# A one-operation reciprocal root in the context LayerNorm, and three more context FFN steps emitted ahead of the reload

## The chip, the cores and the metric

The kernel runs on one core of a Trainium2 chip. The metric is the device time of one execution in microseconds (us), lower is better. All times below come from one profiled execution of the kernel before, or from its three timed runs.

## The reference, cut to what matters

The program is one inference step of a two-layer backbone with two groups of tokens that share all weights: 128 context tokens (`xc`) and 1024 latent tokens (`xl`), of width 1024. Layer 0 mixes tokens with a state-space scan (S5), layer 1 with window pooling. Each layer ends in a SwiGLU FFN of width 2816, and each of the two sub-layers ends in a LayerNorm of the scaled residual.

```python
def layer_norm(x, g, b):
    mu = jnp.mean(xf, axis=-1, keepdims=True)
    var = jnp.mean(jnp.square(xf - mu), axis=-1, keepdims=True)
    y = (xf - mu) * lax.rsqrt(var + LN_EPS)
    return (y * g + b).astype(x.dtype)

def swiglu(h, w_gate, w_up, w_down):
    return (jax.nn.silu(h @ w_gate) * (h @ w_up)) @ w_down

# layer 0, for the context (c) and for the latent tokens (l):
oc, fin_re, fin_im = s5_mixer(hc, *params, zeros, zeros)      # scan, output tables, gelu, GLU
ol, _, _ = s5_mixer(hl, *params, state_re[:, j], state_im[:, j])
xc = layer_norm(DEEPNORM_ALPHA * xc + g1c * oc, ln_g[i, 0], ln_b[i, 0])
xl = layer_norm(DEEPNORM_ALPHA * xl + g1l * ol, ln_g[i, 0], ln_b[i, 0])
fc = swiglu(modulate(xc, sh2c, sc2c), ffn_w_gate[i], ffn_w_up[i], ffn_w_down[i])
fl = swiglu(modulate(xl, sh2l, sc2l), ffn_w_gate[i], ffn_w_up[i], ffn_w_down[i])
```

## The kernel before, in words

Activations lie with the channels on the 128 partitions and the tokens along the free dimension. The context is one block of 128 tokens (`C`), the latent tokens are two blocks of 512 (`A`, `B`). Context matmuls are plain fp32; the profile lists each as two records. Latent matmuls are split into three products of high and low parts (L844 to L846).

In layer 0 the order of the program around the change is this.

- **Scan.** `ssm_scan_lat` runs 127 dependent steps in two directions on VectorE (L477, L482). Beside it, `ctx0a` brings the context through its own GLU and its first LayerNorm (`ln_stats`, `ln_apply`). While `self.scanning` holds, the context's elementwise work goes to GpSimd (`elem`), and what GpSimd needs from PSUM is copied by ScalarE (`in_sb`). The LayerNorm ends in the modulated context `xmc` (L1014), on which every matmul of the context FFN waits. In it the reciprocal of the root is taken by GpSimd as a power of minus one (L993), after a Sqrt on ScalarE (L989); two multiplications by GpSimd then refine it by a Newton step, before (`lr`) and after this change alike.
- **Readout and reload.** `ssm_y` runs eight times (the tiles 6, 7, 5, 0, 1, 2, 3, 4). Each time it loads tables (`mo` of 1 MB into two buffers; `mk` of 0.5 MB), copies scan states into `sd` (L629, L631, L633), multiplies (`py`, L677 and L680), applies gelu on ScalarE (`yl`, L683) and stores to a scratch tensor `yd` (L686). After the last one the main program reloads `yd` in another layout as `yr` (L1200) and splits it (`xm`, `xn`); this is the reload.
- **GLU of the latent blocks.** `glu(A)` and `glu(B)` make eight output tiles each, and after each tile one step is taken from the iterator `fill`.

The context FFN of layer 0 is that iterator, `ctx0b`: 22 steps of `ffn_up` (16 matmuls and two weight loads of 512 KB each), 8 steps of `ffn_down` (22 matmuls each), and the second context LayerNorm at the 31st call. 15 steps are emitted ahead of the reload by `self.step(fill, 15)`; the 16 calls in the two GLUs take the rest. Steps ahead of the reload load their weights into the three buffers of the pool `raw`, those behind it into the small buffers `rc` (256 KB).

The program order is not the order on the engines: a scheduler of the framework with a simulated timeline places each engine's instructions, and every engine then runs its own list strictly in that order. The SyncE queue (SP) issues the loads, also in order. The first six `ffn_up` steps multiply on GpSimd, later ones on VectorE (L918, `hc`).

Of the kernel before, what the change touches and what calls it, by code (L numbers as in the profile page):

```python
# [11 lines left out]
F32 = mybir.dt.float32  # L12
F32R = mybir.dt.float32r
I32 = mybir.dt.int32
AF = mybir.ActivationFunctionType
OP = mybir.AluOpType
# [25 lines left out]
class Kernel:  # L42
# [920 lines left out]
    def ln_stats(self, b):  # L963

        nc = self.nc
        v = self.elem(b)
        n = b.n
        x = b.x
        t = b.tmp.tile([128, 2, n], F32, tag="lt" + b.tg, name="lt", bufs=3)
        v.tensor_tensor(t, x[:, 0:2], x[:, 2:4], op=OP.add)  # L970
        v.tensor_tensor(t, t, x[:, 4:6], op=OP.add)
        v.tensor_tensor(t, t, x[:, 6:8], op=OP.add)
        v.tensor_tensor(t[:, 0], t[:, 0], t[:, 1], op=OP.add)
        pm = self.in_sb(b, v, self.ones_mm(b, t[:, 0], "lnm"))
        acc = None
        for q in range(4):
            xq = x[:, 2 * q:2 * q + 2]
            v.tensor_tensor(xq, xq, pm.unsqueeze(1).to_broadcast([128, 2, n]), op=OP.subtract)
            sq = b.tmp.tile([128, 2, n], F32, tag="lt" + b.tg, name="sq", bufs=3)
            nc.scalar.activation(sq, xq, AF.Square)  # L980
            if acc is None:
                acc = sq
            else:
                v.tensor_tensor(acc, acc, sq, op=OP.add)
        v.tensor_tensor(acc[:, 0], acc[:, 0], acc[:, 1], op=OP.add)
        pv = self.ones_mm(b, acc[:, 0], "lnv")
        r = b.tmp.tile([128, n], F32, tag="lr" + b.tg, name="lr", bufs=1)
        q = b.tmp.tile([128, n], F32, tag="lq" + b.tg, name="lq", bufs=1)
        nc.scalar.activation(q, pv, AF.Sqrt, bias=self.eps if b.split else self.epsc[:, 0:1])  # L989
        if v is nc.vector:  # L990
            v.reciprocal(r, q)
        else:
            v.tensor_tensor(r, q, self.minus.to_broadcast([128, n]), op=OP.pow)  # L993
        self.stt(b, q, pv, LN_EPS / (ALPHA * ALPHA), r, OP.add, OP.mult, self.epsc[:, 0:1])
        self.stt(b, q, q, -0.5, r, OP.mult, OP.mult)
        self.stt(b, r, q, 1.5, r, OP.add, OP.mult)
        for q in range(4):
            xq = x[:, 2 * q:2 * q + 2]
            v.tensor_tensor(xq, xq, r.unsqueeze(1).to_broadcast([128, 2, n]), op=OP.mult)
# [158 lines left out]
    def build(self):  # L1158
        tc, nc = self.tc, self.nc
        with ExitStack() as st:  # L1160
# [15 lines left out]
            self.XC = P("xcres").tile([128, 8, 128], F32, name="XC")  # L1176
            self.gate, self.lnm = {}, {}
            self.scanning = False
            self.minus = self.cp.tile([128, 1], F32, name="minus")
            nc.vector.memset(self.minus, -1.0)  # L1180
            self.ident = self.cp.tile([128, 128], F32, name="ident")
            make_identity(nc, self.ident)
            self.ssm()
            fill = self.ctx0b()
            self.step(fill, 15)
            self.scanning = False
            self.whl = P("whl")
            xr = P("xres")
# [5 lines left out]
            with tc.tile_pool(name="xm1", bufs=1) as xmp:  # L1194
# [20 lines left out]
                with tc.tile_pool(name="adl", bufs=1, side="right") as adl:  # L1215
                    fill = self.ada_late(adl)
# [19 lines left out]
            fill = self.ctx1b()  # L1236
# [91 lines left out]
```

## Time and profile before

| | |
|---|---|
| timed runs | 2452.82, 2456.66, 2459.58 us (median 2456.66) |
| the profiled execution's own time | 2459.29 us |
| its span in the profile | 2457.3 us, 33344 instructions |
| TensorE (PE) busy | 2254.7 us, 92% of the span |
| VectorE (DVE), ScalarE (ACT), GpSimd (POOL) busy | 1281.1, 937.5, 284.2 us |
| mean granted TensorE clock | 0.958 of full speed |

The profiled execution took 2.6 us more than the median of the three runs. A stretch is read as follows: the busy time of each engine in it, the granted clock of TensorE as a share of its full 2.4 GHz, the share of the 16 DMA engines that was busy, and the rate at which they moved data. An instruction is read by its start, its duration, and in square brackets the idle time of its engine just before it and what ended that.

### The profile page before, as it was taken

To read this page: it belongs to the slowest core of one execution; us is meant where nothing else is said; L and a number is where in the kernel's file an instruction comes from. 1 tells how busy PE (TensorE), PEld (TensorE's weight loads), DVE (VectorE), ACT (ScalarE), POOL (GpSimd) and SP (SyncE) were. 2 spreads that over 40 slices of the span, in tenths; PEclk is the share of its full clock that TensorE was granted. 3 is DMA by queue.
4 is the path that set the end of the run, shared out by engine and by line. 5 is a ranking of instruction groups with operands and counts; after the bars stand their busy time and mean duration, and the time that the engine had idled before them with its cause. 6 is when DMAs were issued, how large, how long until landed. Compare 5 with 4: busy or idle time off the path is not lost.

```text
span 2457.3 us, 33344 instructions
## 1 busy us (share of the span) xinstructions
PE 2254.7 (92%) x13105; PEld 1871.8 (76%) x13105; DVE 1281.1 (52%) x2421; ACT 937.5 (38%) x1387; POOL 284.2 (12%) x338
## 2 busy tenths in 40 slices
PE   4896658799999999999999999889999999999996
PEld 2565648688887777788888888777788888888996
DVE  6779962344546222456223765677322456322476
ACT  2774234543225222544222544126222443322464
POOL 4921474300010000100000010001000100000000
PEclk7896879899999999999999999999999999999998
DMA  7877448864554554423333326773333232333452
GB/s 219 243 235 218 138 106 255 246 175 138 162 161 154 158 193 156 168 96 93 102 96 95 103 95 180 213 201 110 104 94 95 97 100 86 98 94 95 143 198 103
DMA packets 458012, 357.22 MB, mean 145 GB/s; under 512 B 14960, under 2 KB 405888, under 8 KB 455808
## 3 DMA queue, kind: packets, MB, share of 16 engines
q1 hardware_dynamic: 451920, 340.91, 46.2%
q0 software_dynamic: 3200, 8.39, 1.1%
q10 hardware_dynamic: 2736, 5.80, 0.6%
q8 instruction: 103, 1.69, 0.3%
q14 instruction: 53, 0.43, 0.1%
HBM read 336.58 MB, written 18.35 MB: 144 GB/s over the span
## 4 chain that ended last, share of the span: by engine, by line
PE 80%; DMA 11%; DVE 3%; ACT 2%; POOL 2%; issue 1%; SPq 0%; ACTq 0%; POOLq 0%; DVEq 0%
PE ffn L844 13%; PE ffn L846 13%; PE ffn L845 13%; PE dn L844 6%; PE dn L845 6%; PE dn L846 6%; PE ffn L848 4%; PE dn L848 3%; PE glu L845 2%; PE glu L846 2%; PE glu L844 2%; DMA adaw<-ada_w 2%; DMA raw<-ffn_w_gate 2%; DMA raw<-ffn_w_down 1%; DMA mo<-mo 1%
## 5 line engine op out<-in xcount | busy, mean ns | idle before, releaser
L828 ACT ACTIVATE wh<-raw 128x1024 fp32r<-128x1024 f32 (+1 forms) x326 | 341.5, 1049 | 947.7 <-PE ffn L845 623.4
L829 DVE TENSOR_TENSOR wl<-raw,wh 128x1024 fp32r<-128x1024 f32 (+1 forms) x326 | 394.3, 1210 | 500.1 <-ACT wh L828 491.8
L845 PE MATMUL dn<-hkl,wh 128*128 128x512 f32 (+1 forms) x880 | 304.5, 348 | 0.3 <-DVE hkl L829 0.3
L846 PE MATMUL dn<-hkh,wl 128*128 128x512 f32 (+1 forms) x880 | 302.9, 347 | 0.0
L844 PE MATMUL ffn<-xp,wh 128*128 128x512 f32 x704 | 280.3, 398 | 2.2 <-ACT wh L828 2.2
L846 PE MATMUL ffn<-xp,wl 128*128 128x512 f32 x704 | 280.0, 398 | 0.5 <-DVE wl L829 0.5
L845 PE MATMUL ffn<-xp,wh 128*128 128x512 f32 x704 | 279.9, 398 | 0.0
L844 PE MATMUL ffn<-xm,wh 128*128 128x512 f32 x704 | 274.4, 391 | 1.2 <-ACT xm L828 0.7
L846 PE MATMUL ffn<-xm,wl 128*128 128x512 f32 x704 | 274.8, 391 | 0.0
L845 PE MATMUL ffn<-xm,wh 128*128 128x512 f32 x704 | 274.8, 390 | 0.0
L844 PE MATMUL dn<-hkh,wh 128*128 128x512 f32 (+1 forms) x880 | 262.5, 348 | 0.9 <-ACT hkh L828 0.9
L848 PE MATMUL ffn<-xmc,raw 128*128 128x128 f32 x1184 | 154.3, 287 | 53.4 <-POOL xmc L1014 28.2
L918 DVE TENSOR_TENSOR h<-ffn,sg 128x512 f32<-128x512 f32 x88 | 60.6, 689 | 256.0 <-PE ffn L846 255.4
L848 PEld LDWEIGHTS ffn<-xmc,raw 128*128 128x128 f32 x1184 | 146.5, 201 | 61.7 <-POOL xmc L1014 28.5
L845 PEld LDWEIGHTS dn<-hkl,wh 128*128 128x128 f32 x880 | 166.6, 189 | 21.1 <-DVE hkl L829 0.5
L846 PEld LDWEIGHTS dn<-hkh,wl 128*128 128x128 f32 x880 | 166.5, 189 | 20.5
L844 PEld LDWEIGHTS dn<-hkh,wh 128*128 128x128 f32 x880 | 163.2, 189 | 23.3 <-ACT hkh L828 1.7
L844 PEld LDWEIGHTS ffn<-xp,wh 128*128 128x128 f32 x704 | 133.0, 189 | 35.1 <-ACT wh L828 2.5
L846 PEld LDWEIGHTS ffn<-xp,wl 128*128 128x128 f32 x704 | 132.9, 189 | 33.6 <-DVE wl L829 1.0
L845 PEld LDWEIGHTS ffn<-xp,wh 128*128 128x128 f32 x704 | 133.0, 189 | 32.5 <-issue 0.7
L844 PEld LDWEIGHTS ffn<-xm,wh 128*128 128x128 f32 x704 | 132.0, 188 | 33.2 <-issue 3.8
L846 PEld LDWEIGHTS ffn<-xm,wl 128*128 128x128 f32 x704 | 132.1, 188 | 28.8 <-issue 1.5
(333 smaller groups left out, 3328.2 us busy)
## 6 DMA issues: line engine op xcount, KB each, us to landing
raw<-ffn_w_down SPq DMA_DIRECT2D x126, 512.0 KB
raw<-ffn_w_gate SPq DMA_DIRECT2D x125, 512.0 KB
raw<-ffn_w_up SPq DMA_DIRECT2D x125, 512.0 KB
adaw<-ada_w SPq DMA_DIRECT2D x96, 512.0 KB
raw<-ssm_glu_w SPq DMA_DIRECT2D x48, 512.0 KB
mo<-mo SPq DMA_DIRECT2D x14, 1024.0 KB
rc<-ffn_w_down SPq DMA_DIRECT2D x40, 256.0 KB
mo<-otab SPq DMA_DIRECT2D x32, 256.0 KB
```

The lines of the kernel that those rows point to most:

```text
L828: nc.scalar.activation(h, src, AF.Copy)
L829: nc.vector.tensor_tensor(l, src, h.bitcast(F32), op=OP.subtract)
L844: nc.tensor.matmul(ps, wh, xh, start=start, stop=False)
L845: nc.tensor.matmul(ps, wh, xl, start=False, stop=False)
L846: nc.tensor.matmul(ps, wl, xh, start=False, stop=stop)
L848: nc.tensor.matmul(ps, w[0], x[0], start=start, stop=stop)
L918: v.tensor_tensor(h[:, f, :], self.in_sb(b, v, pu), sg, op=OP.mult)
```

## The change

In `ln_stats`, the context block that runs on GpSimd takes its reciprocal root from one ScalarE operation, straight from the PSUM sum; the Sqrt, the power and the constant tile `minus` go. Blocks on VectorE keep Sqrt and reciprocal. In `build`, three more steps of the context FFN are emitted ahead of the reload, so that 18 stand there and 13 calls in the two GLUs take what is left.

```diff
@@ ln_stats
-        nc.scalar.activation(q, pv, AF.Sqrt, bias=self.eps if b.split else self.epsc[:, 0:1])
+        eps = self.eps if b.split else self.epsc[:, 0:1]
         if v is nc.vector:
+            nc.scalar.activation(q, pv, AF.Sqrt, bias=eps)
             v.reciprocal(r, q)
         else:
-            v.tensor_tensor(r, q, self.minus.to_broadcast([128, n]), op=OP.pow)
+            nc.scalar.activation(r, pv, AF.Abs_reciprocal_sqrt, bias=eps)
@@ build
-            self.minus = self.cp.tile([128, 1], F32, name="minus")
-            nc.vector.memset(self.minus, -1.0)
...
             fill = self.ctx0b()
-            self.step(fill, 15)
+            self.step(fill, 18)
```

The instructions move in three places of layer 0. The lines of the changed program are numbered one higher than before from L995 to the `minus` lines.

**GpSimd, end of the first context LayerNorm.** `sq` is the sum of squares, `lr` the reciprocal root, `xmc` the modulated context, `hc` the gated FFN activation, `sd` a copy of scan states. Before:

```order
L985 TENSOR_TENSOR sq<-sq 128x128
L993 TENSOR_TENSOR lr<-lq,minus 128x128
L890 TENSOR_TENSOR lq<-st,lr 128x128
L889 TENSOR_SCALAR st<-lq 128x128
L890 TENSOR_TENSOR lq<-st,lr 128x128
L889 TENSOR_SCALAR st<-lq 128x128
L890 TENSOR_TENSOR lr<-st,lr 128x128
L999 TENSOR_TENSOR XC<-XC,lr 128x256 x4
L1014 TENSOR_SCALAR xmc<-XC,lnm_2905 128x128 x8
L631 COPY sd<-Z_568 64x512
L918 TENSOR_TENSOR hc<-cp,sg 128x128 x2
```

Now:

```order
L985 TENSOR_TENSOR sq<-sq 128x128
L890 TENSOR_TENSOR lq<-st,lr 128x128
L889 TENSOR_SCALAR st<-lq 128x128
L890 TENSOR_TENSOR lq<-st,lr 128x128
L889 TENSOR_SCALAR st<-lq 128x128
L890 TENSOR_TENSOR lr<-st,lr 128x128
L1000 TENSOR_TENSOR XC<-XC,lr 128x256 x4
L1015 TENSOR_SCALAR xmc<-XC,lnm_2903 128x128 x8
L918 TENSOR_TENSOR hc<-cp,sg 128x128 x6
L631 COPY sd<-Z_566 64x512
```

The power is gone from GpSimd, and all six FFN products that GpSimd makes stand ahead of its first copy of scan states.

**TensorE, from the same LayerNorm to the first readouts.** `ffn` with `raw` are the context FFN's steps ahead of the reload, `py` the readout of the scan. Before:

```order
L960 MATMUL lnv<-sq,ones 128x128
L848 MATMUL ffn<-xmc,raw 128x128 x24
L680 MATMUL py_3974<-sd,mo 128x128
L848 MATMUL ffn<-xmc,raw 128x128 x8
L680 MATMUL py_3975<-sd,mo 128x128
L848 MATMUL ffn<-xmc,raw 128x128 x23
L680 MATMUL py_3974<-sd,mo 128x128
```

Now:

```order
L960 MATMUL lnv<-sq,ones 128x128
L848 MATMUL ffn<-xmc,raw 128x128 x136
L680 MATMUL py_3971<-sd,mo 128x128
L680 MATMUL py_3972<-sd,mo 128x128
L848 MATMUL ffn<-xmc,raw 128x128 x23
L680 MATMUL py_3971<-sd,mo 128x128
```

136 matmuls (8.5 steps) stand ahead of the first readout where 24 (1.5 steps) stood. From the end of the readout of tile 6 to the end of that of tile 2 there are 7.6 steps where there were 8.1, and behind that 0.5 where there were 3.4.

**VectorE, near the end of the scan.** `stt` and `Z` are the scan's product and state of the backward direction. Before:

```order
L477 TENSOR_TENSOR stt_366<-rm,Z_572 128x128
L482 TENSOR_TENSOR Z_572<-stt_366,Z_572 128x64 x2
L477 TENSOR_TENSOR stt_366<-rm,Z_572 128x128
L482 TENSOR_TENSOR Z_572<-stt_366,Z_572 128x64 x2
L477 TENSOR_TENSOR stt_366<-rm,Z_572 128x128
```

Now:

```order
L477 TENSOR_TENSOR stt_364<-rm,Z_570 128x128
L482 TENSOR_TENSOR Z_570<-stt_364,Z_570 128x64 x2
L477 TENSOR_TENSOR stt_364<-rm,Z_570 128x128
L918 TENSOR_TENSOR hc<-ffn,sg 128x128
L482 TENSOR_TENSOR Z_570<-stt_364,Z_570 128x64 x2
L477 TENSOR_TENSOR stt_364<-rm,Z_570 128x128
```

That is the product of the FFN's step 8; it stands in the scan with between three and four backward steps to come. The product of step 7 stands seven backward steps ahead of the scan's end.

## Rows read from the trace of the kernel before

**Rows 1.** Chain that ended last, around the context LayerNorm: start, us, what

```profile
303.58 0.81 PE lnv L960 x2
304.86 20.87 POOL lr L993
...
332.60 5.94 PE ffn L848 x30
```

**Rows 2.** Stretches (from:to, length): busy us (instructions) of PE, PEld, DVE, ACT, POOL; clock; DMA share; GB/s

```profile
292.00:333.00 41.00, 2.00 (x6) 1.41 (x7) 40.87 (x193) 4.28 (x9) 37.44 (x27) 0.51 0.06 17
...
340.00:456.00 116.00, 96.68 (x811) 94.44 (x810) 35.70 (x40) 60.50 (x76) 56.92 (x79) 0.96 0.87 245
...
497.00:620.00 123.00, 120.70 (x655) 104.22 (x655) 53.67 (x58) 53.40 (x60) 0.43 (x1) 0.99 0.54 156
620.00:740.00 120.00, 119.34 (x679) 102.30 (x678) 53.68 (x69) 32.73 (x44) 9.90 (x8) 1.00 0.53 157
```

**Rows 3.** ScalarE in order of time, end of the context LayerNorm

```profile
301.74 1.28 ACT L989 ACT_TABLE_LOAD   x1
304.42 0.37 ACT L989 ACTIVATE lq<-lnv,epsc 128x128 f32<-128x128 f32 x1 [1.40 <-PE lnv L960]
```

**Rows 4.** SyncE queue in order of time: first context FFN load that waited, 512 KB

```profile
338.55 0.37 SPq L837 DMA_DIRECT2D raw<-ffn_w_up  x1
```

**Rows 5.** The context's GLU, weights of the same size streamed alone; columns as rows 2

```profile
262.00:268.00 6.00, 4.97 (x45) 4.81 (x44) 6.00 (x34) 1.06 (x4) 2.04 (x4) 1.00 1.01 261
268.00:274.00 6.00, 4.94 (x43) 4.59 (x41) 6.00 (x32) 0.81 (x3) 2.79 (x5) 1.00 0.84 240
274.00:280.00 6.00, 5.24 (x47) 5.07 (x46) 6.00 (x33) 0.62 (x2) 2.45 (x5) 1.00 0.82 234
280.00:286.00 6.00, 4.82 (x39) 4.29 (x38) 6.00 (x36) 0.62 (x2) 1.73 (x3) 1.00 0.84 237
```

**Rows 6.** TensorE in order of time, first FFN steps and readouts of tile 6

```profile
340.37 0.39 PE L680 MATMUL py<-sd,mo 128*128 128x128 f32 x2
342.37 2.05 PE L848 MATMUL ffn<-xmc,raw 128*128 128x128 f32 x16 [1.61 <-DMA raw<-ffn_w_up]
...
351.61 0.39 PE L680 MATMUL py<-sd,mo 128*128 128x128 f32 x2
```

**Rows 7.** VectorE in order of time, a scan step beside the power; end of the scan

```profile
322.52 0.48 DVE L477 TENSOR_TENSOR stt<-rm,Z 128x128 f32<-128x128 f32 x2
...
323.47 0.48 DVE L477 TENSOR_TENSOR stt<-rm,Z 128x128 f32<-128x128 f32 x2
...
337.77 0.48 DVE L482 TENSOR_TENSOR Z<-stt,Z 128x64 f32<-128x64 f32 x2
338.29 2.92 DVE L633 COPY sd<-Z 64x512 f32<-64x512 f32 x4
```

**Rows 8.** VectorE in order of time, copies for the last two readouts, tiles 3 and 4

```profile
428.73 4.41 DVE L633 COPY sd<-Z 64x512 f32<-64x512 f32 x4 [7.68 <-PE py L680]
...
441.07 3.03 DVE L633 COPY sd<-Z 64x512 f32<-64x512 f32 x3 [3.31 <-PE py L680]
```

**Rows 9.** TensorE in order of time, last readout

```profile
450.64 0.61 PE L680 MATMUL py<-sd,mo 128*128 128x128 f32 x4
```

**Rows 10.** ScalarE in order of time, last readout

```profile
450.84 2.00 ACT L828 ACTIVATE wh<-raw 128x1024 fp32r<-128x1024 f32 x2 [1.51 <-DMA raw<-ssm_glu_w]
452.87 1.28 ACT L683 ACT_TABLE_LOAD   x1
454.16 0.60 ACT L683 ACTIVATE yl<-py 128x512 f32<-128x512 f32 x1
```

**Rows 11.** Tile `rc`: the FFN steps inside the latent GLUs

```profile
L848 PE MATMUL ffn<-xmc,rc x224: 270/275/582, 464.2 to 591.1; 128*128 128x128 f32 x112
```

**Rows 12.** Chain that ended last: context matmuls inside the latent GLUs

```profile
597.76 2.68 PE dn L848 x24
```

## The prediction

> **What bounds the kernel now.** I read the chain of waits first, then the busy time by stretch, then each engine's timeline around the change. In the chain [rows 1] the power on GpSimd stands alone for 20.87 us, from 304.86 to 325.7, and the first matmul of the context FFN starts at 332.60. The stretches [rows 2] show four stages with different limits. From 292 to 333 TensorE is busy 2 of 41 us and the DMA engines 6%: the weights of the next 1.5 steps are loaded, no buffer comes free, and only the scan on VectorE moves. From 340 to 456, the readout with 13.5 FFN steps between, the DMA engines are busy 87% at 245 GB/s and TensorE 96.7 of 116 us: transfers set the pace. Then the reload runs, and from 497 to 740 TensorE is busy 120.7 of 123 and 119.3 of 120 us: there every matmul costs its own time. So the change has three prices: a wait that goes, loads and matmuls that move into an empty stretch, and matmuls that leave a full one.
>
> **The reciprocal root.** ScalarE's Sqrt takes 0.37 us, and its table load of 1.28 us is over before the sum arrives, with 1.40 us of waiting left [rows 3]. The new list has one table load and one operation in that place too. No row shows the new function. Nothing speaks for less than Sqrt; above, one more load on the path would add 1.3 us. I take 0.37, since shape, source and engine are those of Sqrt. GpSimd then goes on at 304.9 where it went on at 325.7: `xmc` and the first FFN matmul come 20.9 us earlier, at 311.7. The memset that goes is at the program's start and is taken as nothing.
>
> **What the new order does with 20.9 us.** The first load that waits for a free buffer is issued at 338.55 [rows 4]; it will be issued near 317.7. Now 136 matmuls stand ahead of the first readout; 24 have their weights, so 14 loads of 512 KB must come first. Their pace: in the context's GLU, loads of that size stream alone at 261, 240, 234 and 237 GB/s [rows 5], mean 243, or 2.16 us a load and 4.3 a step. The first takes 3.8 us from issue to its matmuls (338.55 to 342.37), and a half step of 16 records 2.05 us [rows 4, 6]. So the 136th matmul ends at 317.7 + 3.8 + 13 x 2.16 + 2.05 = 351.6, where the first readout stood at 340.37 [rows 6]. 23 more matmuls (2.9 loads, 6.2 us) follow, so the main part of tile 6 starts at 357.8 and not at 351.61: 6.2 us later.
>
> **The wait that is added.** VectorE's products of steps 7 and 8 stand inside the scan. A scan step takes 0.95 us beside the power (322.52 to 323.47), and the scan ends at 338.25 [rows 7]. By the pace above step 7 ends at 345.1 and step 8 at 349.5, so VectorE stands still in the scan from about 331. Behind step 8 come 3.5 scan steps (3.3 us) and 2.9 us of copies [rows 7], till about 356. TensorE asks for them at 357.8, so the wait is covered, by 2 us only. Both hang on the same step 8, so a slower stream delays both; without the cover each us would cost one. GpSimd's and ScalarE's copies queue behind FFN products in the same way and under the same cover. On the SyncE queue the table loads for the third readout now stand behind more weight loads, but they wait for tile 6's readout to free a buffer in any case.
>
> **When the reload starts.** Two sums. By bytes: 116 us x 245 GB/s is 28.4 MB [rows 2]; six more loads add 3.1. 31.5 MB at 244 GB/s take 129 us from 319.1 (340 - 20.9), till about 448.5: 7.5 us before 456. By steps: 6.2 us later at tile 6; then 0.56 fewer steps to tile 2, -2.4 us; then the last two readouts, which took from 428.73 to 451.25 [rows 8, 9] with 3.4 steps among them, have 0.5. If loads set their pace, 2.9 steps x 4.3 = 12.5 us go; if their own chain of copies, table loads and gelu does, nothing. I take 7.5, which leaves 15 us for two readouts with copies of 4.4 us each [rows 8]. Last, the gelu that ends the stage now runs at 454.16, 2.9 us after its matmul, behind a weight split and a table load [rows 9, 10]; in the new list that table load is gone and the split stands ahead. 6.2 - 2.4 - 7.5 - 2.9 = -6.6. The sums agree; I take 7 us, between 0.9 later (tail gains nothing) and 11.6 earlier.
>
> **The latent GLUs.** Of the seven up-steps there (224 records [rows 11]) four remain: 3 x 16 matmuls of two records leave, 96 records at 2.68/24 = 0.112 us [rows 12] = 10.7 us. TensorE is full there [rows 2], so all of it counts. The new order has the 13 remaining calls start as before and leaves the last three tiles of the second GLU without FFN work. The context LayerNorm moves into the GLU with its table switch; ScalarE is busy 32.7 of 120 us there, so I cost it at nothing. I keep 9 to 10.7.
>
> **The sum** against the profiled execution: 2459.29 - 7 - 10.7 = 2441.6. That execution was 2.6 us above the median of the three runs, so for the median I predict 2456.66 - 17.7 = **2439 us**.
>
> **The clock of the stream.** At 332.60 the first 30 records took 5.94 us, 0.198 each [rows 1], against 0.112 later [rows 12]: the lower of the two levels, 1.2 GHz, after TensorE had been all but idle (0.51 granted from 292 to 333 [rows 2]). I take the full level for the stream behind its first us, because in the context's GLU, with the same waits for loads and TensorE busy 4.8 to 5.2 of every 6 us, the granted clock was 1.00 [rows 5]. At the lower level a step would take 32 x 0.198 = 6.3 us and TensorE, not the loads, would set the pace. The Trainium skill (TensorE: Matmul & The Clock Gate, "HAM oscillation — how this bites in real kernels") tells of a kernel whose short groups of matmuls wait for a load in each tile of K and fall back to the lower clock every time; by it the stream would be the third rival below. The trace disagrees for the waits that it has.
>
> **Rivals.**
> - *The readout gains nothing.* The stream delays tile 6, and the readouts keep a pace of their own. For it: TensorE now reaches the first readout 11 us later; in the last two readouts VectorE waited for TensorE and not for loads [rows 8]. Against: 87% DMA. The reload starts 1 us late or up to 4, and only the GLU's 10.7 remain: 2446 to 2450. Chance 0.13.
> - *More fits into the empty stretch.* At the 261 GB/s of the first of [rows 5], 31.5 MB end near 440, 16 us early: 2456.7 - 26.7 = 2430. Against: the rows behind it are lower. Chance 0.09.
> - *The clock stays low* (slower). It decides where it outlasts the stream: 159 matmuls are 318 records, 63 us, so tile 6 starts at 374.7, 23.1 us late; the 12.8 gained behind it leave 10.3, which the GLU's 10.7 cancel: 2456, as before. Any readout still at that level makes it slower; 40 us of further matmuls at 0.198 for 0.112 cost some 30 us less the slack of a sixth: 2475. I put 2465. Chance 0.06.
> - *The change is not what it says*: the lists show the power gone, one root operation and three steps moved. Only a costlier table load is left, 1.3 us, inside the range.
>
> **How the numbers follow.** The forecast, a reload 3 to 12 us earlier with 9 to 10.7 saved behind it, spans 2434 to 2445 and has 0.72. The range takes in the fast rival and most of the first: 2430 to 2450. 0.3%, about what a measurement of this kernel can tell from no change, is 7.4 us (2449.3 and 2464.0). Faster: forecast, fast rival and most of the first, 0.86; within: the rest of the first and part of the clock case, 0.09; slower 0.05.
>
> **What would show it.** Right: no power row; first FFN matmul near 312; DMA near 240 GB/s from 319 to 352; first `py` near 352 with VectorE idle in the scan; last gelu near 447; TensorE still full in the GLUs; no FFN records in the last three tiles. Wrong: granted clock near 0.5 from 320 to 350; a main readout of tile 6 that waits for `sd`; a last gelu at 455 or later.

## The result, and the profile after

The changed kernel takes 2424.04 us (median of four runs, 2420.78 to 2432.99) where the kernel before took 2455.76 in the same measurement (median of four): a ratio of 0.9876, 95% interval 0.9845 to 0.9906. That is 31.7 us faster. The prediction was 17.7 us, and the time lies below its range.

Up to the readout the profile after has what was forecast. ScalarE at the end of the LayerNorm (start us, us, line, operation, what it waited for), where [rows 3] stood:

```profile
302.64 1.28 ACT L994 ACT_TABLE_LOAD   x1
305.32 0.37 ACT L994 ACTIVATE lr<-lnv,epsc 128x128 f32<-128x128 f32 x1 [1.40 <-PE lnv L960]
```

One table load, one root of 0.37 us, the same wait of 1.40 us. GpSimd goes on at once, in place of the power's 20.87 us in [rows 1]:

```profile
306.02 0.46 POOL L890 TENSOR_TENSOR lq<-st,lr 128x128 f32<-128x128 f32 x1 [1.59 <-ACT st L887]
```

TensorE after, the first FFN matmuls and the first two readouts, where [rows 6] stood:

```profile
312.49 8.02 PE L848 MATMUL ffn<-xmc,raw 128*128 128x128 f32 x48 [7.21 <-POOL xmc L1015]
...
353.99 0.61 PE L680 MATMUL py<-sd,mo 128*128 128x128 f32 x4
...
360.69 0.39 PE L680 MATMUL py<-sd,mo 128*128 128x128 f32 x2
```

The SyncE queue's first load that waited for a buffer ([rows 4] before):

```profile
318.53 0.37 SPq L837 DMA_DIRECT2D raw<-ffn_w_up  x1
```

First matmul 312.49 (forecast 311.7), first waiting load 318.53 (317.7), first readout 353.99 (351.6), main part of tile 6 at 360.69 (357.8). VectorE in the scan, with the copies behind it ([rows 7] before):

```profile
347.77 0.29 DVE L918 TENSOR_TENSOR hc<-ffn,sg 128x128 f32<-128x128 f32 x1 [15.57 <-ACT sg L916]
...
352.38 0.28 DVE L918 TENSOR_TENSOR hc<-ffn,sg 128x128 f32<-128x128 f32 x1
...
355.63 4.40 DVE L633 COPY sd<-Z 64x512 f32<-64x512 f32 x4
```

VectorE stands still from 332.2 to 347.8 for step 7, the wait that the change adds, and its copies end at 360.0; TensorE begins tile 6 at 360.69. The busy time by stretch (us, then busy us and instructions of PE, PEld, DVE, ACT, POOL, the granted clock, the DMA share, GB/s), to be held against [rows 2]:

```profile
312.00:340.00 28.00, 23.19 (x173) 22.18 (x174) 20.20 (x119) 7.45 (x19) 6.88 (x13) 0.90 0.60 170
319.00:352.00 33.00, 27.19 (x222) 25.29 (x220) 17.19 (x93) 5.33 (x16) 3.89 (x7) 1.00 0.80 229
340.00:440.00 100.00, 89.66 (x723) 87.00 (x722) 41.26 (x65) 49.46 (x60) 48.54 (x61) 0.93 0.85 247
440.00:482.00 42.00, 25.78 (x160) 23.29 (x159) 14.17 (x14) 16.78 (x22) 14.74 (x26) 0.80 0.71 215
482.00:600.00 118.00, 113.30 (x627) 97.35 (x627) 44.46 (x50) 43.68 (x51) 1.59 (x3) 1.00 0.58 173
600.00:720.00 120.00, 119.42 (x633) 101.41 (x633) 67.60 (x85) 42.45 (x56) 8.58 (x6) 1.00 0.48 144
```

The second row, which overlaps its neighbours, is the stream alone, from the first waiting load to the first readout. The empty stretch is filled, and the GLUs are as full as before. ScalarE at the end of the readout stage ([rows 10] before), with the reload's first split:

```profile
446.60 0.60 ACT L683 ACTIVATE yl<-py 128x512 f32<-128x512 f32 x1 [4.05 <-DMA yd<-yl]
...
448.34 2.00 ACT L828 ACTIVATE wh<-raw 128x1024 fp32r<-128x1024 f32 x2 [1.14 <-PE py L677]
450.25 0.58 ACT L683 ACTIVATE yl<-py 128x512 f32<-128x512 f32 x1
...
465.43 1.13 ACT L828 ACTIVATE xm<-yr 128x512 fp32r<-128x512 f32 x1 [14.61 <-DMA yr<-yd]
```

The last gelu runs at 450.25, 3.9 us earlier than in [rows 10]; the forecast had it near 447. The last two readouts, between the start of VectorE's copies for the first of them and the end of TensorE's last `py` ([rows 8, 9] before):

```profile
433.99 4.42 DVE L633 COPY sd<-Z 64x512 f32<-64x512 f32 x4 [9.28 <-PE py L680]
...
448.14 0.61 PE L680 MATMUL py<-sd,mo 128*128 128x128 f32 x4
```

**Where the other half is.** I cut both traces at TensorE's landmarks: first `py`, first `glu<-xm`, last `glu<-xn`, first and last `ffn<-xm` (layer-0 latent FFN), first context `ffn` of layer 1, first and last `ffn<-xp` (layer-1 latent FFN), end. A last matmul counts to its end. Before and after, in us:

| stretch | before | after | difference |
|---|---|---|---|
| start to first `py` | 254.8 | 255.5 | +0.7 |
| to the reload (first `glu<-xm`) | 217.5 | 212.4 | -5.1 |
| the two latent GLUs | 254.0 | 244.3 | -9.7 |
| `ffn<-xm`, first to last | 633.5 | 631.0 | -2.5 |
| to the context FFN of layer 1 | 108.6 | 108.6 | 0 |
| context FFN of layer 1, to the first `ffn<-xp` | 202.9 | 202.1 | -0.8 |
| `ffn<-xp`, first to last | 625.8 | 610.6 | **-15.2** |
| to the end | 160.4 | 159.6 | -0.8 |

The first rows are the predicted mechanism: 17.3 us by the three stretches that it reaches (5.1 + 9.7 + 2.5), in one profile of each kernel. The 15.2 us lie some 940 us behind the GLUs, the last stretch in which the diff moves an instruction. The groups of TensorE by line and form say how (busy us, mean ns of one, idle time). Before:

```profile
L844 PE MATMUL ffn<-xp,wh 128*128 128x512 f32 x704 | 280.3, 398 | 2.2 <-ACT wh L828 2.2
L846 PE MATMUL ffn<-xp,wl 128*128 128x512 f32 x704 | 280.0, 398 | 0.5 <-DVE wl L829 0.5
L845 PE MATMUL ffn<-xp,wh 128*128 128x512 f32 x704 | 279.9, 398 | 0.0
L846 PE MATMUL ffn<-xm,wl 128*128 128x512 f32 x704 | 274.8, 391 | 0.0
```

After:

```profile
L846 PE MATMUL ffn<-xp,wl 128*128 128x512 f32 x704 | 275.3, 391 | 0.5 <-DVE wl L829 0.5
...
L846 PE MATMUL ffn<-xm,wl 128*128 128x512 f32 x704 | 275.0, 391 | 0.0
L844 PE MATMUL ffn<-xp,wh 128*128 128x512 f32 x704 | 274.8, 391 | 2.2 <-ACT wh L828 2.2
...
L845 PE MATMUL ffn<-xp,wh 128*128 128x512 f32 x704 | 274.6, 391 | 0.0
```

No wait went. The 2112 matmuls of this group became 7 ns shorter in the mean (398 to 391), 2112 x 0.007 = 15 us, and now take what the same shape takes in layer 0, in both kernels. A record overlaps the next one, so its length is not the pace; but the pace changed by as much, from 233 to 227 ns between one start and the next (means, with the 22 and 15 pauses of 300 ns and more left out). The granted clock is no answer: it is 1.00 from 1800 to 2296 us before, and from 1780 to 2264 after.

**What else the change moves.** The diff deletes a tile, `minus`, one column of 4 bytes in the constants' pool. In the compiled program it held 32 bytes of each partition, so every left-hand tile behind it begins 32 bytes lower after the change: the pieces `wh` of the weights at 38016 in place of 38048 (`wl` 12288 = 48 x 256 bytes behind them), `xm` at 128128 in place of 128160, `h2` at 137344 in place of 137376. The pool of `xp` hangs on the other side: 185216 in both. So weights and `xm` kept their distance, weights and `xp` did not. Addresses are bytes within a partition, as the compiled program has them.

### The profile page after: what moved, and what is told of

It reads as the page before. It is cut to its first block, busy times and chain, and to the rows that moved or that the text cites. A ratio compares the mean times of both kernels' runs of the same rounds, so it can differ in the third digit from the quotient of the medians.

```text
span 2424.1 us, 33331 instructions
## 1 busy us (share of the span) xinstructions
PE 2243.9 (93%) x13105; PEld 1872.7 (77%) x13105; DVE 1282.3 (53%) x2420; ACT 922.9 (38%) x1376; POOL 269.1 (11%) x337
## 4 chain that ended last, share of the span: by engine, by line
PE 81%; DMA 11%; DVE 3%; ACT 2%; issue 1%; POOL 1%; SPq 0%; ACTq 0%; POOLq 0%; DVEq 0%
PE ffn L844 13%; PE ffn L846 13%; PE ffn L845 13%; PE dn L845 6%; PE dn L844 6%; PE dn L846 6%; PE ffn L848 4%; PE dn L848 3%; PE glu L844 2%; PE glu L846 2%; PE glu L845 2%; DMA adaw<-ada_w 2%; DMA raw<-ffn_w_up 2%; DMA raw<-ffn_w_gate 1%; PE pvv L465 1%
## 5 line engine op out<-in xcount | busy, mean ns | idle before, releaser
L828 ACT ACTIVATE wh<-raw 128x1024 fp32r<-128x1024 f32 (+1 forms) x326 | 341.6, 1049 | 930.4 <-PE ffn L845 611.4
L846 PE MATMUL dn<-hkh,wl 128*128 128x512 f32 (+1 forms) x880 | 303.0, 347 | 0.0
L844 PE MATMUL ffn<-xp,wh 128*128 128x512 f32 x704 | 274.8, 391 | 2.2 <-ACT wh L828 2.2
L846 PE MATMUL ffn<-xp,wl 128*128 128x512 f32 x704 | 275.3, 391 | 0.5 <-DVE wl L829 0.5
L844 PE MATMUL ffn<-xm,wh 128*128 128x512 f32 x704 | 275.2, 392 | 0.0
L846 PE MATMUL ffn<-xm,wl 128*128 128x512 f32 x704 | 275.0, 391 | 0.0
L845 PE MATMUL ffn<-xp,wh 128*128 128x512 f32 x704 | 274.6, 391 | 0.0
L844 PE MATMUL dn<-hkh,wh 128*128 128x512 f32 (+1 forms) x880 | 262.5, 348 | 0.9 <-ACT hkh L828 0.9
L848 PE MATMUL ffn<-xmc,raw 128*128 128x128 f32 x1280 | 166.3, 287 | 33.7 <-DMA raw<-ffn_w_up 9.9
L848 PEld LDWEIGHTS ffn<-xmc,raw 128*128 128x128 f32 x1280 | 157.2, 200 | 43.9 <-DMA raw<-ffn_w_up 13.7
L846 PEld LDWEIGHTS dn<-hkh,wl 128*128 128x128 f32 x880 | 166.5, 189 | 20.4
L844 PEld LDWEIGHTS dn<-hkh,wh 128*128 128x128 f32 x880 | 163.3, 189 | 23.4 <-ACT hkh L828 1.7
L844 PEld LDWEIGHTS ffn<-xm,wh 128*128 128x128 f32 x704 | 132.1, 188 | 31.8 <-issue 4.3
L844 PEld LDWEIGHTS ffn<-xp,wh 128*128 128x128 f32 x704 | 132.5, 188 | 30.7 <-ACT wh L828 2.5
L846 PEld LDWEIGHTS ffn<-xp,wl 128*128 128x128 f32 x704 | 132.5, 188 | 28.9 <-DVE wl L829 1.0
L846 PEld LDWEIGHTS ffn<-xm,wl 128*128 128x128 f32 x704 | 132.1, 188 | 28.9 <-issue 0.7
## 6 DMA issues: line engine op xcount, KB each, us to landing
rc<-ffn_w_down SPq DMA_DIRECT2D x40, 256.0 KB
mo<-otab SPq DMA_DIRECT2D x32, 256.0 KB
```

The source lines that it names most:

```text
L828: nc.scalar.activation(h, src, AF.Copy)
L844: nc.tensor.matmul(ps, wh, xh, start=start, stop=False)
L845: nc.tensor.matmul(ps, wh, xl, start=False, stop=False)
L846: nc.tensor.matmul(ps, wl, xh, start=False, stop=stop)
L848: nc.tensor.matmul(ps, w[0], x[0], start=start, stop=stop)
```

## The experiments

In the tile view, the figures behind the colon are ns, shortest, median and longest, then the first and the last start in us and the shape, counted in every fourth record. One line of the three (L844 to L846) stands for all. The kernel before, then the changed kernel:

```profile
L844 PE MATMUL ffn<-xp,wh x704: 389/396/796, 1671.2 to 2296.0; 128*128 128x512 f32 x176
```

```profile
L844 PE MATMUL ffn<-xp,wh x704: 387/389/799, 1653.9 to 2263.7; 128*128 128x512 f32 x176
```

Runs E5 to E7 and E9 to E11 have one timed execution each, in which stretches paced by transfers differ by some us (table at the end); there the pace of the matmuls is what is read.

**E1, the changed kernel with a pad in the place of `minus`.**

```diff
+self.pad = self.cp.tile([128, 8], F32, name="pad")
+nc.vector.memset(self.pad, 0.0)
 self.ident = self.cp.tile([128, 128], F32, name="ident")
```

> The changed kernel with an unused 128 x 8 tile (32 bytes a partition) put where the one-column tile of minus ones stood, so that every tile behind it, the weight pieces among them, begins 32 bytes further on, as before the change; the order of the work is the changed kernel's. Theory P (place): in the layer-1 latent FFN a matmul took 396 ns before and 389 after because the weight pieces (address 38048 before, 38016 after) and the input tiles xp (185216 in both) then stand at different remainders by 64 bytes. It expects 396 ns again, the last ffn<-xp matmul about 15 us later than in the changed kernel, and 2424 + 15 = 2439 us. Theory S (schedule): the pace comes from what is emitted beside these matmuls. It expects 389 ns and 2424 us. Theory V (variation from one build or chip to another): no forecast for one run, but it would not follow the pads in run after run.

```profile
L844 PE MATMUL ffn<-xp,wh x704: 392/396/797, 1653.1 to 2276.8; 128*128 128x512 f32 x176
```

2441.69 us, 0.9932 of the kernel before (0.9906 to 0.9958). In the compiled program every other tile lies where it lay before the change. The unused 32 bytes bring 396 ns and 14 us of `ffn<-xp` back, with the changed kernel's order of work. So the place decides, and this run is the change without its side effect: 15.8 us faster than before.

**E2, the kernel before with `xp` 32 bytes lower.**

```diff
 xm = [xmp.tile([128, 8, 512], F32R, name=f"xp{q}") for q in range(2)]
+shift = xmp.tile([128, 8], F32, name="shift")
+nc.vector.memset(shift, 0.0)
```

> The kernel before, with an unused 32-byte tile added to the pool of the layer-1 inputs, so that the two xp tiles begin 32 bytes lower (185184 in place of 185216) and nothing else moves; pow, the tile of minus ones and 15 steps stay. Theory P expects 389 ns for ffn<-xp in place of 396, since weights and inputs then share their remainder by 64 bytes, and 2456 - 15 = 2441 us. Theory S expects 396 ns and 2456 us: the order of work is that of before.

```profile
L844 PE MATMUL ffn<-xp,wh x704: 391/394/794, 1676.6 to 2301.4; 128*128 128x512 f32 x176
```

2454.97 us, 0.999 (0.9972 to 1.0009): nothing gained. Equal remainders by 64 bytes are not the rule; theory P fell in that form.

**E3, the root alone (15 steps, `minus` gone), and E4, the steps alone (18 steps, pow and `minus` kept).**

```diff
# E3, against the changed kernel
-self.step(fill, 18)
+self.step(fill, 15)
# E4, against the kernel before
-self.step(fill, 15)
+self.step(fill, 18)
```

> The changed kernel with 15 steps ahead of the reload in place of 18: the reciprocal root on ScalarE and the tile of minus ones gone. Mechanism as predicted: the first FFN matmul at 312.5 us as in the changed kernel, but three steps fewer (3 x 4.4 us by the changed kernel's step time) end them near 341 us, where before they ended at 340.4, so the readout stage and the reload stay where they were before within 2 us, and the GLU keeps its 96 more records. Theory P adds the layer-1 pace, 389 ns and 15 us: 2456 - 15 = 2441 us, between 2436 and 2443. Theory S, if the pace hangs on the three steps: 396 ns and 2454 to 2457 us.

> The kernel before with 18 steps in place of 15: pow on GpSimd and the tile of minus ones stay. Mechanism as predicted: the first FFN matmul stays at 332.6 us, the 18 steps end some 13 us later than before, at 354 + 20 = 374 us against 354 in the changed kernel, the readout behind them ends 10 to 16 us later than in the changed kernel, and the GLU gives back 10 to 11 us by 96 records fewer. Theory P: 396 ns stays. Sum: 2456 + 10 to 2456 - 2, so 2454 to 2466 us. Theory S, if the pace hangs on the three steps: 389 ns and 15 us less, 2439 to 2451 us.

E3:

```profile
L844 PE MATMUL ffn<-xp,wh x704: 387/389/800, 1671.2 to 2282.8; 128*128 128x512 f32 x176
```

E4:

```profile
L844 PE MATMUL ffn<-xp,wh x704: 389/396/797, 1659.9 to 2282.0; 128*128 128x512 f32 x176
```

E3: 2438.62 us, 0.9922 (0.9898 to 0.9946). E4: 2447.79 us, 0.9963 (0.9944 to 0.9982). The pace goes with the tile and not with the steps, so theory S is out. Both runs also correct my picture of the steps. In E3 the readout did not stay where it was: 318 FFN matmul records stand ahead of tile 6's main part, as many as in the changed kernel, and tile 6 starts at 361.5. The scheduler had put the 15 steps early and the last 36 us of readouts (413 to 449) without any; the stage's last `py` still ended 193.6 us after the first, against 193.2 with 18 steps. So the three steps ran in gaps of the last readouts (96 records between 411.6 and 437 us after the change) and cost nothing that can be told from the spread: five profiles with the changed kernel's order and 18 steps have 193.2 to 196.2 us there (the changed kernel, E1, E5, E10, E11). In E4 the order of before stayed, with 48 records ahead of the first readout and not 272; of the 96 added records 16 went ahead of the readout's end and the rest into the wait of the reload, which starts 5.5 us later (223.0 against 217.5), and the GLUs are 12.8 us shorter. My forecast for E4 (2454 to 2466) was 6 us too slow at its nearer end. The parts add up: the steps alone give 9.7 us, the root alone 18.9, of which 13.3 are `ffn<-xp`'s; 9.7 + 5.6 = 15.3, by E1's 15.8. The last two readouts of E3, with no FFN step among them:

```profile
432.80 4.35 DVE L633 COPY sd<-Z 64x512 f32<-64x512 f32 x4 [8.64 <-issue]
...
448.74 0.61 PE L680 MATMUL py<-sd,mo 128*128 128x128 f32 x4
```

**E5 to E7 and E11, other distances between weights and `xp`.** The edit is that of E2 with 8 columns (E5, on the changed kernel), 24 (E6) and 56 (E7, both on the kernel before), and 48 (E11, on the changed kernel).

> The changed kernel with the two xp tiles 32 bytes lower (185184 in place of 185216), the weight pieces left at 38016, nothing else moved. The first runs leave this of theory P: the pace of ffn<-xp goes with the place of the tiles and not with the steps, but equal remainders by 64 bytes (the kernel before with xp moved, 38048 and 185184) did not bring 389 ns back. Theory P128: the distance from the weight pieces to the moving tile has to be a multiple of 128 bytes (or of 256). Distances seen: 90112 = 704 x 128 in layer 0 (389 ns), 147200 = 1150 x 128 in the changed kernel (389), 147168 and 147136, neither a multiple, in the two slow ones (396). Here it is 147168: P128 expects 395 to 396 ns, and 13 to 15 us more than 2424. Theory W: only the place of the weight pieces and of the tiles that move with them (h2, raw) counts, not that of xp. It expects 389 ns and 2424 us.

> The kernel before with the xp tiles 96 bytes lower (185120), so that the distance from the weight pieces (38048) is 147072 = 1149 x 128 bytes, an odd multiple of 128; pow and the tile of minus ones stay. P128 expects 389 ns in ffn<-xp and 2457 - 15 = 2442 us. The same with 256 in place of 128 expects 396 ns and 2457 us, and so does theory W.

> The kernel before with the xp tiles 224 bytes lower (184992): the distance is 146944 = 574 x 256 bytes, a multiple of 128, 256 and 512. P128 and the same with 256 or 512 expect 389 ns and 2442 us; theory W expects 396 ns and 2457 us.

> The changed kernel with the xp tiles 192 bytes lower (185024): the distance from the weight pieces is 147008 = 574 x 256 + 64 bytes. Distances past a multiple of 256 seen so far: 0 (389 ns), 128 (mean 395), 192 and 224 (395 to 396). P256 expects 394 to 396 ns for 64 and some 2437 us; the rival that only distances past the middle of the 256 bytes cost expects 389 ns and 2424 us.

E5, E6, E7 and E11 in this order:

```profile
L844 PE MATMUL ffn<-xp,wh x704: 392/396/796, 1650.7 to 2275.3; 128*128 128x512 f32 x176
```

```profile
L844 PE MATMUL ffn<-xp,wh x704: 387/393/800, 1674.1 to 2296.9; 128*128 128x512 f32 x176
```

```profile
L844 PE MATMUL ffn<-xp,wh x704: 386/390/800, 1667.7 to 2277.8; 128*128 128x512 f32 x176
```

```profile
L844 PE MATMUL ffn<-xp,wh x704: 388/394/792, 1651.2 to 2270.2; 128*128 128x512 f32 x176
```

E5: 2437.29 us, E6: 2459.45, E7: 2439.95, E11: 2432.35. Moving `xp` alone by 32 bytes makes the changed kernel slow (E5), and 224 bytes make the kernel before fast with pow and `minus` still in it (E7: 610.9 us from the first to the last `ffn<-xp`, against 625.8). An odd multiple of 128 does not do (E6). 147200 = 575 x 256 of the changed kernel is no multiple of 512 and is fast, so of these distances it is the multiples of 256 bytes that are fast. E11 (64 past a multiple) is slow, but by less: 619.8 us, with a mean of 397 ns in the first block (1730 to 1880 us) and 391 in the second (2080 to 2230). What sets the size of the cost stays open.

**E9, the same in layer 0, and E10, `h2` in its old place.**

```diff
# E9
+gap = xmp.tile([128, 8], F32, name="gap")
+nc.vector.memset(gap, 0.0)
 xm = [xmp.tile([128, 8, 512], F32R, name=f"xm{q}") for q in range(2)]
# E10
+gap = P("gap").tile([128, 8], F32, name="gap")
+nc.vector.memset(gap, 0.0)
 hp = tc.tile_pool(name="ffnb", bufs=1)
```

> The changed kernel with an unused 32-byte tile ahead of the layer-0 inputs xm, so that these (and the GLU's xn behind them) begin at 128160 in place of 128128; weight pieces and xp stay. Theory P256 (a matmul takes 389 ns when weight piece and moving tile stand a multiple of 256 bytes apart, 395 or so when not) says that the same holds in layer 0: ffn<-xm goes from 389 to 395 to 396 ns, ffn<-xp stays at 389, and the time rises by 2112 x 6 ns = 13 us in layer 0 and 2 x 384 x 6 ns = up to 5 us in the GLU, to 2437 to 2442 us. A rival that ties the effect to the layer-1 stage (its xp tiles, or what runs beside it) expects 389 ns in both and 2424 us.

> The changed kernel with an unused 32-byte tile ahead of h2, the layer-1 products that VectorE writes: h2 begins at 137376, as in the kernel before, in place of 137344; weight pieces and xp stay where the change has them. h2 is the other tile of that stage whose place the change moved. P256 expects 389 ns in ffn<-xp and 2424 us; the rival that h2's place counts expects 395 ns and 2437 us.

E9, tile `xm`, then tile `xp`; then E10, tile `xp`:

```profile
L844 PE MATMUL ffn<-xm,wh x704: 388/396/792, 723.9 to 1367.2; 128*128 128x512 f32 x176
```

```profile
L844 PE MATMUL ffn<-xp,wh x704: 387/389/799, 1683.3 to 2293.0; 128*128 128x512 f32 x176
```

```profile
L844 PE MATMUL ffn<-xp,wh x704: 387/389/799, 1662.4 to 2274.1; 128*128 128x512 f32 x176
```

E9: 2454.9 us, 13 us above the forecast's upper end. `ffn<-xm` goes to 396 and `ffn<-xp` stays at 389: the effect belongs to the pair of tiles and not to layer 1. Of the 29 us over the changed kernel's span, `ffn<-xm` has 13.2 and the GLUs 5.5, close to the forecast for these two; the rest lies before the first `py` (3.2), between it and the reload (3.1) and in layer 1's context FFN (4.5), stretches that differ by as much between other profiles. E10: 389 ns, so `h2` does not count. Its one time, 2436.94 us, is what the rival forecast, but the table shows the reason elsewhere: 2.7 us before the reload, 5.9 in layer 1's context FFN.

**E8, 20 steps.**

```diff
-self.step(fill, 18)
+self.step(fill, 20)
```

> The changed kernel with 20 steps ahead of the reload. From 15 to 18 steps (root alone against the changed kernel) the GLU stage, first glu<-xm to last glu<-xn, fell from 256.0 to 244.2 us (3.9 us a step), the layer-0 FFN's first half from 267.4 to 264.9, and the reload did not come later (469.4 and 468.0). Theory K (the readout's end is set by its own copies and transfers, and the steps fill PE's idle time before it): two steps more give 2 x 3.9 = 8 us, 2416 us. Theory L (the steps now wait for their weights, 4.4 us each, and push the readout): the reload comes up to 2 x 4.4 = 9 us later, and it ends within 2 us of 2424.

2421.79 us, 0.9859 (0.9838 to 0.988). The GLUs are 5.6 us shorter where theory K had 8, and the reload comes 4.9 us later behind the first `py` (1.5 later than in the slowest profile with 18 steps in this order): in kind theory L, though the time lies 0.2 us below its band. The interval overlaps the changed kernel's, so this is no better version that could be told from it.

**E12, the added wait taken away.**

```diff
-v = self.elem(b, f < 6)
+v = self.elem(b, f < 8)
```

> The changed kernel with the products of FFN steps 7 and 8 on GpSimd as well (the first eight steps in place of the first six), which takes the added wait out of VectorE's scan: in the changed kernel it stood from 332.2 to 347.8 us waiting for step 7. Theory C (covered, as predicted): the scan ends near 339 in place of 355.6, but the readout of tile 6 still follows the eighteenth step's last matmul on TensorE, at 358 to 362 us, and the time is 2424 us within 4. Theory U (the wait costs): the readout stage starts or ends earlier by 3 us or more, and the time is 2417 to 2421 us. A price of its own would show as GpSimd's products queueing in front of its copies for the readout.

VectorE, end of the scan and its copies, then TensorE, main part of tile 6:

```profile
340.03 0.48 DVE L482 TENSOR_TENSOR Z<-stt,Z 128x64 f32<-128x64 f32 x2
340.55 2.92 DVE L633 COPY sd<-Z 64x512 f32<-64x512 f32 x4
362.39 0.29 DVE L918 TENSOR_TENSOR hc<-ffn,sg 128x128 f32<-128x128 f32 x1 [18.91 <-ACT sg L916]
```

```profile
365.74 0.39 PE L680 MATMUL py<-sd,mo 128*128 128x128 f32 x2
365.96 0.39 PE L677 MATMUL py<-u,mk 128*128 128x128 f32 x2
```

2431.79 us, 0.989 (0.9872 to 0.9908). The scan ends 15 us earlier and its copies 17, and tile 6 starts 105.5 us after the first `py`, where the changed kernel has 105.2. So the wait was covered, theory C for the start; the time is no better, and 3.8 us above the upper end of C's band, with an interval that overlaps the changed kernel's. Its profile is 4.8 us later than the changed kernel's at the first `py`, ahead of all that was edited, and loses 4.6 more from there to the reload; why is not settled.

The landmarks of all runs, us. "Past 256" is the distance from weight pieces to `xp`, less a multiple of 256 bytes (to `xm` it is 0 everywhere but in E9, where it is 32).

| run | past 256 | first `py` to reload | GLUs | `ffn<-xm` | context FFN, layer 1 | `ffn<-xp` | span |
|---|---|---|---|---|---|---|---|
| before | 224 | 217.5 | 254.0 | 633.5 | 202.9 | 625.8 | 2457.3 |
| after | 0 | 212.4 | 244.3 | 631.0 | 202.1 | 610.6 | 2424.1 |
| E1 | 224 | 212.5 | 242.1 | 631.1 | 205.9 | 624.6 | 2437.5 |
| E2 | 192 | 221.4 | 252.2 | 633.5 | 203.7 | 625.7 | 2461.8 |
| E3 | 0 | 213.7 | 256.0 | 633.5 | 203.8 | 612.5 | 2442.7 |
| E4 | 224 | 223.0 | 241.2 | 631.0 | 201.8 | 623.0 | 2441.9 |
| E5 | 224 | 212.0 | 244.3 | 631.0 | 198.8 | 625.5 | 2435.5 |
| E6 | 128 | 215.0 | 254.6 | 633.5 | 204.8 | 623.6 | 2457.5 |
| E7 | 0 | 215.1 | 252.2 | 634.0 | 201.3 | 610.9 | 2437.9 |
| E8 | 0 | 217.3 | 238.7 | 631.0 | 197.9 | 611.4 | 2421.7 |
| E9 | 0 | 215.5 | 249.8 | 644.2 | 206.6 | 610.5 | 2453.1 |
| E10 | 0 | 215.1 | 243.2 | 630.9 | 208.0 | 612.5 | 2435.2 |
| E11 | 64 | 215.8 | 241.7 | 630.9 | 201.5 | 619.8 | 2430.6 |
| E12 | 0 | 217.0 | 241.9 | 630.9 | 200.6 | 612.2 | 2431.3 |

Profiles with one order of work differ too. From the first `py` to the reload the four with the order of before (before, E2, E6, E7) have 215.0 to 221.4 us, the six with the changed kernel's (after, E1, E5, E9, E10, E11) 212.0 to 215.8. By the means of the two groups the change gives 3.4 us there, 10.1 in the GLUs and 2.6 in `ffn<-xm` (E9 left out of the last two): 16.1 us, by E1's 15.8.

## Why the prediction was right and wrong

**The step that failed** is one sentence: "The memset that goes is at the program's start and is taken as nothing." The memset is nothing. The tile that it filled is not: its removal moves every tile behind it, and one pair of operands came to stand 575 x 256 bytes apart. The sum had no term for that, and no rival. It is worth 15.2 us in the trace, 14.0 us of `ffn<-xp` in E1, and 14.9 in E7, which has none of the change's intended parts. Without it (E1) the change gives 15.8 us, 2441.7, inside the stated range and 2.7 us from the forecast. Part of that nearness is luck: the reload gave less than its term, and a stretch that the sum left out gave about as much more.

**The reciprocal root**: right. 0.37 us, one table load, the first FFN matmul 20.1 us earlier for 20.9 predicted; the matmul that sums the squares ahead of the root itself came 0.9 us later (304.49 for 303.58).

**The stream**: right in kind, a little fast. 353.99 for 351.6 and 360.69 for 357.8. The first waiting load came 0.8 us late, and by the prediction's own sum a load took (353.99 - 318.53 - 3.8 - 2.05) / 13 = 2.28 us for 2.16.

**The added wait**: right, and tighter than said. VectorE stood still from 332.2 (331 predicted) to 347.8 (345.1), copies ended at 360.0 (356), 0.7 us ahead of TensorE in place of 2. E12 shows the cover by taking the wait away.

**The reload**: right in sign, half the size. The 7 us were 3.7 at the reload's first split (469.08 to 465.43). The largest term came true: the last two readouts took 22.5 us before (428.73 to 451.25) and 14.8 after (433.99 to 448.75), 7.8 us less for 7.5. E3's took 16.6 (432.80 to 449.35) with no FFN step among them and 224 GB/s in place of 247 from 340 to 440, so 15 us and more is what they need by themselves. Mis-sized were the other terms. Tile 6 came 9.1 us later for 6.2, and the last two readouts began 5.3 us later for 3.8. And the gelu gave 1.4 us for 2.9: the weight split that the sum put out of its way starts at 448.34 and still stands in front of it, so it runs 1.5 us after the last matmul. 5.3 - 7.8 - 1.4 = -3.9. The first rival had the delay of tile 6 in kind; its claim that the readouts gain nothing is not borne out.

**The GLU term**: 9 to 10.7 predicted, 9.7 in the GLUs and 2.5 more in the first half of the layer-0 FFN (267.4 to 264.9 us from the first `ffn<-xm` to the first `dn`), which the sum had left out. In the kernel before the context's second LayerNorm still ran in that stretch; the 2.5 us were not taken apart further.

**The other rivals.** "More fits into the empty stretch" named a time near the measured one (2430) for a reason that the trace refutes: 229 GB/s from 319 to 352 and not 261. "The clock stays low" did not happen: the first 48 records took 8.02 us, 0.167 each, but from 319 to 352 us the granted clock was 1.00, and 0.93 from 340 to 440, where 1.2 GHz throughout would read 0.5. The prediction let the Trainium skill (TensorE: Matmul & The Clock Gate, "HAM oscillation — how this bites in real kernels") speak for this rival. The kernel of that page waits some 3 to 5 us for each load; the stream's waits for loads were 0.2 to 2.0 us, so the page's case is not this one.

## What to carry to other kernels

When a change adds, drops or resizes a tile, compare the addresses of all operands of the long matmul groups before and after, and read the mean duration of each group in both traces: a pace that changes without a wait is a term that no chain of waits shows. Here weight pieces and moving tile a multiple of 256 bytes apart gave 389 ns a matmul and the other distances tried 392 to 396, so an allocation can be checked for that, and padded; other shapes and types were not tried. To judge an edit by itself, keep the places of the other tiles with a pad, as E1 does.

## What the runs showed of the hardware

A 128 x 512 matmul of the split kind depends on where its two SBUF operands stand to each other. Ten placements of weights and `xp` or `xm` were seen. In the four with a distance of 0 past a multiple of 256 bytes the median was 389 to 390 ns, at absolute addresses that differ; in the six with 32, 64, 128, 192 and 224 (twice) it was 392 to 396. The weight load's own record does not change (188 ns in both). The raw loads' buffers and other left-hand tiles moved together with the weight pieces, so a write to one of those might be the partner in place of TensorE's own weight reads. A stretch in which VectorE, ScalarE, GpSimd and the DMA engines all stand still says no. Before, then after: the stretch, and two starts of the same line 18 matmuls apart:

```profile
1728.50:1733.30 4.80, 4.80 (x23) 3.84 (x22) 0.00 (x0) 0.00 (x0) 0.00 (x0) 1.00 0.00 0
...
1728.24 0.40 PE L844 MATMUL ffn<-xp,wh 128*128 128x512 f32 x1
...
1732.44 0.40 PE L844 MATMUL ffn<-xp,wh 128*128 128x512 f32 x1
```

```profile
1708.70:1713.20 4.50, 4.50 (x23) 3.71 (x21) 0.00 (x0) 0.00 (x0) 0.00 (x0) 1.00 0.00 0
...
1708.44 0.39 PE L845 MATMUL ffn<-xp,wh 128*128 128x512 f32 x1
...
1712.52 0.39 PE L845 MATMUL ffn<-xp,wh 128*128 128x512 f32 x1
```

That is a start every 233 ns before and every 227 after, the whole difference, with nothing but TensorE at work on SBUF. That its partner is the weights rests on these matmuls reading no other SBUF tile; moving the weights alone was not tried. The mechanism is not shown.

The Trainium skill (SBUF — State Buffer, "A bandwidth-pool intuition that's wrong (but worth ruling out)") gives TensorE a second, independent read port for weight loads; by it the distance should not matter. The measurement differs: where the distance is no multiple of 256 bytes, a layer's up and gate matmuls took 9 to 15 us longer than the changed kernel's 610.6 us or, in layer 0, its 631.0. Here the measurement decides.
